# Sample step, block inverse and first memory attention as background jobs beside five projections; value transposes directly behind their projection

## The chip, the cores and the metric

The kernel runs on one core of a Trainium2 chip. The metric is the device time of one execution in microseconds (us). A core has five engines with an instruction queue each: TensorE (PE in the rows; PEld is its weight load), VectorE (DVE), ScalarE (ACT), GpSimd (POOL) and SyncE (SP). Transfers are issued from a queue of SP or ACT.

## What is computed

One step of a decoder trunk of two layers for a prompt of 1024 positions and a sample group of 8 single positions, with the same weights; all 1032 columns go through each projection together, in three chunks of 352, 336 and 344. Layer 0 is the "even" one: gated delta rule (4 heads of 128), dilated attention in windows, and attention over a memory of 256 entries. Layer 1 is the "odd" one: a linear recurrence (RG-LRU) and a memory attention of its own.

```
x0 = prompt and sample
for layer in (0, 1):
    h   = rms_norm(x) * g_pre
    kv  = rms_norm(mem) @ w_mem_kv                  # keys and values of the memory
    mix = concat(branches(h @ w_in), memory_attend(q, kv) * silu(gate))
    x   = x + rms_norm(mix @ w_out) * g_post

# gated delta rule, prompt: chunks of 128
a_low = (beta k k^T) * strict_lower * decay
u, w  = solve(a_low + I, [beta v, beta k exp(g)])   # block inverse, then two levels of joining
for each chunk: v' = u - w S;  o = q S + attn v';  S = decay S + k^T v'

# gated delta rule, sample: one position for each of 8 states
S = exp(g) S;  u = (v - k^T S) beta;  S = S + k u^T;  o = q^T S
```

The outputs are both groups' rows of the last layer, the new states and caches, and the memory's keys and values.

## The kernel before

The kernel is written against a tile framework that schedules: instructions are traced in program order, and each engine's queue is then filled from what is ready, earlier program text first, so that later projections can move ahead of a stalled part. Each engine works its own queue in order. `tc.high_priority(offset=HP)` puts a block ahead of all others. Matrix products of projections are split into three passes of fp32r operands (high x high, low x high, high x low: L164 to L166), 8 blocks of 128 rows each: 24 matmuls for a chunk. A projection is `proj` (weights cast to a high and a low part on ACT and GpSimd, L152 and L154; then, for each chunk, matmuls into a PSUM tile of bank group `p`, the drain that the caller gives, and `tick()`).

`start(lane, steps)` puts a generator on a lane; each `tick()` lets every lane take one portion. What a portion issues is pinned behind the last instruction traced so far on each engine, so that it can't be scheduled earlier than that. `yield n` in a job means a pause of n ticks. `drain_lanes` ticks until the lanes named are empty. `at_once` traces a generator's steps on the spot, unpinned.

The part of layer 0 that matters stands in `even_gdn`'s second half. The preparation of the delta rule writes the chunk matrices to DRAM (`aqd`). Then, in program text: the block inverse of 128 blocks of 32x32 (16 loads `bl` L752 on SP; 31 rows, each with a product `tm` L758 over i*i elements and a sum `xi` L760, both on DVE; a transposed copy L761 and two stores L762 and L763), under high priority; the sample step (convolution of 4 taps, norms, 64 small matmuls `gks` L803, the update `u`, two transposes, and for each of the 8 states a spread `gum` L831 on GpSimd, a matmul `gou` L834, four scalings L837 on ACT, an addition `gst` L838 on DVE and a store L839 issued by ACT; the states are loaded by ACT's queue); the first memory head, `mem_head(0)` (query projection wq00, gate projection wg00, attention `mem_attend` with L375 to L402, store of `mix`); `mem_scaled`, a product for layer 1's memory norm; and three projections taken ahead for the windowed attention, `swa_ahead` (gate wb0, keys/queries ws010 and ws000). These draw their result tiles `pa` from pool `me` under the tags `qm`, `gm`, `mm`, which are also the tags of the attention's query, gate and mix, one buffer each. Drains L520 and L523 are ACT copies into `pa`, L526 is the copy of the sample columns on DVE. After that the bank groups of PSUM are cut anew (L854), and the recurrence proper begins: for each head `chain(h)` loads the inverse from `xd`, joins blocks (`gz` L881, `gt` L886, `gx` L891) and scans the chunks, with the next heads' projections (wq01, wg01, wz0, wq02, ...) beside it.

Layer 1's memory keys and values, `mem_kv(1, ...)`, run at the end of layer 0's output (`out_layer`), beside the norm of the third column chunk (lane "norm2"). For each of four heads a value projection `mv` is drained to a tile `vf` (two buffers, L323), stored, and turned by two transposes L346 and a copy L347 on DVE into `vt`. In layer 1 these turns are a lane of their own, "turn", emptied behind the memory part.

Of the kernel before, what the change touches and what calls it, by code (L numbers as in the profile page):

```python
# [15 lines left out]
P = 128  # L16
# [49 lines left out]
def body(ctx, tc, I, O):  # L66
# [251 lines left out]
    def mem_kv(l, mem, pool, part=None):  # L318
# [17 lines left out]
        for h in range(4 if part != 0 else 0):  # L336
# [13 lines left out]
            if l:  # L350
                start("turn", turn())
            else:
                at_once(turn())
# [201 lines left out]
    def even_gdn(x, prep, sprep):  # L555
        with ExitStack() as es:
# [191 lines left out]
            with tc.high_priority(offset=HP):  # L748
# [6 lines left out]
                V.memset(xi.rearrange("p j i -> p (j i)")[:, 0:1024:33], 1.0)  # L755
                for i in range(1, 32):
                    t3 = tm[:, :i * i].rearrange("p (c j) -> p c j", c=i)
                    V.tensor_tensor(t3, bl[:, 0:i, i][:, None, :].broadcast_to([P, i, i]),  # L758
                                    xi[:, 0:i, 0:i].rearrange("p j c -> p c j"), ALU.mult)
                    V.tensor_reduce(xi[:, i, 0:i], t3, axis=AX.X, op=ALU.add, negate=True)  # L760
                V.tensor_copy(xt.rearrange("p c i -> p i c"), xi)  # L761
                nc.sync.dma_start(out=xd[0].rearrange("h c m j i -> (h c m) (j i)"), in_=xi.rearrange("p j i -> p (j i)"))  # L762
                nc.sync.dma_start(out=xd[1].rearrange("h c m j i -> (h c m) (j i)"), in_=xt.rearrange("p j i -> p (j i)"))  # L763
            nc.scalar.dma_start(out=O["gcp"], in_=gcp)
# [3 lines left out]


            G.tensor_copy(cst_s[:, 3], gpre)  # L770
            nc.scalar.dma_start(out=O["gcs"], in_=cst_s[:, 1:4])
            sc = t3p.tile([P, 12, 8], F32, name="gsc")
            sc2 = t3p.tile([P, 12, 8], F32, name="gsc2")
            wv = vc("gconv", 0, 48).rearrange("p (t j) -> p t j", j=4)
            for j in range(4):
                d = sc if j == 0 else sc2
                V.tensor_tensor(d, cst_s[:, j], wv[:, :, j:j + 1].broadcast_to([P, 12, 8]), ALU.mult)
                if j:
                    V.tensor_tensor(sc, sc, sc2, ALU.add)
            S.activation(sc2, sc, AF.Tanh, scale=0.5)  # L780
            V.scalar_tensor_tensor(sc, sc2, 1.0, sc, ALU.add, ALU.mult)
            V.tensor_tensor(sc2, sc, sc, ALU.mult)
            ps = ctile("gsn")
            T.matmul(ps[:, 0:64], ones, sc2[:, 0:8, :].rearrange("p t b -> p (t b)"), start=True, stop=True)
            nr = t3p.tile([P, 3, 64], F32, name="gnr")
            V.tensor_scalar(nr[:, 0], ps[:, 0:64], 0.25, EPS, op0=ALU.mult, op1=ALU.add)
            rsqrt(nr[:, 1], nr[:, 0], nr[:, 2])
            kq = t3p.tile([P, 4, 8, 2], F32, name="gkq")
            n1 = nr[:, 1].rearrange("p (t b) -> p t b", b=8)
            V.scalar_tensor_tensor(kq[:, :, :, 1], sc[:, 0:4], 0.5 * SC, n1[:, 0:4], ALU.mult, ALU.mult)  # L790
            V.scalar_tensor_tensor(kq[:, :, :, 0], sc[:, 4:8], 0.5, n1[:, 4:8], ALU.mult, ALU.mult)
            ks_ps = ctile("gks")

            sts = []
            for b in range(8):
                t = t3p.tile([P, 4, P], F32, name=f"gst{b}")
                nc.scalar.dma_start(out=t, in_=I["state_gdn"][0, b].rearrange("h k v -> k h v"))
                sts.append(t)
            for b in range(8):
                st = sts[b]  # L800
                for h in range(4):
                    o = (h * 8 + b) * 2
                    T.matmul(ks_ps[:, o:o + 2], st[:, h, :], kq[:, h, b, :], start=True, stop=True)  # L803
            qkp = t3p.tile([P, 4, 8], F32, name="gqkp")
            V.tensor_tensor(qkp, kq[:, :, :, 0], kq[:, :, :, 1], ALU.mult)
            T.matmul(ks_ps[:, 64:96], ones, qkp.rearrange("p h b -> p (h b)"), start=True, stop=True)
            u = t3p.tile([P, 4, 8], F32, name="gu")
            k4 = ks_ps[:, 0:64].rearrange("p (h b t) -> p h b t", h=4, t=2)
            V.tensor_tensor(u, k4[:, :, :, 0], brow[:, 1], ALU.mult)
            V.scalar_tensor_tensor(u, sc[:, 8:12], 0.5, u, ALU.mult, ALU.subtract)  # L810
            V.tensor_tensor(u, u, brow[:, 0], ALU.mult)
            V.tensor_tensor(os_, k4[:, :, :, 1], brow[:, 1], ALU.mult)
            V.tensor_tensor(qkp, u, ks_ps[:, 64:96].rearrange("p (h b) -> p h b", h=4), ALU.mult)
            V.tensor_tensor(os_, os_, qkp, ALU.add)

            rep3 = t3p.tile([P, 2, 3, 4, 8], F32, name="grep3")
            for i in range(3):
                G.tensor_copy(rep3[:, 0, i], kq[:, :, :, 0])
                G.tensor_copy(rep3[:, 1, i], u)
            ps = ctile("grw")  # L820
            for i in range(2):
                T.transpose(ps[0:96, i * P:(i + 1) * P], rep3[:, i].rearrange("p a h b -> p (a h b)"), ident)
            kr_ = t3p.tile([96, P], F32R, name="gkr")
            ur = t3p.tile([96, P], F32R, name="gur")
            V.tensor_copy(kr_, ps[0:96, 0:P])
            V.tensor_copy(ur, ps[0:96, P:256])
            V.tensor_tensor(kr_[64:96], ps[64:96, 0:P], kr_[64:96], ALU.subtract)
            V.tensor_tensor(ur[32:64], ps[32:64, P:256], ur[32:64], ALU.subtract)
            for b in range(8):
                um = t3p.tile([96, 4, P], F32R, name=f"gum{b}", tag="gum", bufs=2)  # L830
                G.tensor_tensor(um, ur[:, None, :].broadcast_to([96, 4, P]),  # L831
                                C("rep32")[0:96, b:32:8][:, :, None].broadcast_to([96, 4, P]), ALU.mult)
                ps = ctile(f"gou{b}")
                T.matmul(ps, kr_, um.rearrange("p h d -> p (h d)"), start=True, stop=True)  # L834
                st = sts[b]
                for h in range(4):
                    S.activation(st[:, h, :], st[:, h, :], AF.Copy, scale=brow[:, 1, h, b:b + 1])  # L837
                V.tensor_tensor(st, st, ps.rearrange("p (h d) -> p h d", h=4), ALU.add)  # L838
                nc.scalar.dma_start(out=O["gdn_s"][b].rearrange("h k v -> k h v"), in_=st)  # L839

            V.tensor_tensor(qkp, os_, os_, ALU.mult)
            ps = ctile("gon")
            T.matmul(ps[:, 0:32], ones, qkp.rearrange("p h b -> p (h b)"), start=True, stop=True)
            V.tensor_scalar(nr[:, 0, 0:32], ps[:, 0:32], 1.0 / 128.0, EPS, op0=ALU.mult, op1=ALU.add)
            rsqrt(nr[:, 1, 0:32], nr[:, 0, 0:32], nr[:, 2, 0:32])
            V.tensor_tensor(os_, os_, nr[:, 1, 0:32].rearrange("p (h b) -> p h b", h=4), ALU.mult)
# [806 lines left out]
```

## Time and profile before

| | |
|---|---|
| three runs | 1916.27, 1918.96, 1923.78 us (median 1918.96) |
| profiled execution | 1920.67 us; span on the core 1918.9 |
| TensorE busy | 1782.3 us, 93% of the span, 11341 matmuls |
| VectorE, ScalarE, GpSimd busy | 1088.6, 715.0, 550.6 us |
| mean granted TensorE clock | 0.954 of full speed |

The profiled execution's time has 1.8 us outside its span. Start times in the rows count from the span's start. [...] In a row on waits: the waiting engine and line, the releaser, total us, times, the longest. In a row in order of time: start, duration, engine, line, operation, output <- inputs, and in brackets the idle time of that engine before it with its releaser.

### The profile page before, as it was taken

How to read it: one execution, taken by the hardware profiler on the slowest of the kernel's cores; microseconds unless marked ns; L12 is line 12 of the kernel's file. 1: busy time of each engine (PE TensorE's matmuls, PEld its weight loads, DVE VectorE, ACT ScalarE, POOL GpSimd, SP SyncE). 2: the span in 40 equal slices, each digit the busy share in tenths (PEclk: the TensorE clock that was granted, in tenths of full speed). 3: DMA queues.
4: the chain of work that ended last, by engine and by line, in shares of the span. 5: the costliest groups of instructions: out<-in, count | busy, mean ns of one | idle time of the engine just before them, and what ended most of it. 6: DMA issues, size and time to landing. Idle time of an engine off the chain costs nothing.

```text
span 1918.9 us, 29175 instructions
## 1 busy us (share of the span) xinstructions
PE 1782.3 (93%) x11341; PEld 1724.7 (90%) x11341; DVE 1088.6 (57%) x2302; ACT 715.0 (37%) x1610; POOL 550.6 (29%) x367
## 2 busy tenths in 40 slices
PE   7999998798999899999999988998499999989996
PEld 6799998698999899999999977998499999988995
DVE  6878759534543314525336376578735647667536
ACT  5355533122322244333333342344223434526432
POOL 3422224222121113231533403215431534331201
PEclk9999998899999899999999998997699999999998
DMA  8435455543344435545644535465633433223554
GB/s 290 180 132 194 181 165 191 193 135 109 114 179 167 177 137 183 205 149 188 213 168 171 169 118 150 131 202 183 234 108 135 143 133 105 84 67 122 152 186 139
DMA packets 160698, 306.25 MB, mean 160 GB/s; under 512 B 25072, under 2 KB 120496, under 8 KB 158640
## 3 DMA queue, kind: packets, MB, share of 16 engines
q1 hardware_dynamic: 67024, 222.47, 33.7%
q10 hardware_dynamic: 93536, 81.93, 13.2%
q8 instruction: 89, 1.46, 0.3%
q14 instruction: 49, 0.40, 0.1%
HBM read 254.05 MB, written 138.28 MB: 204 GB/s over the span
## 4 chain that ended last, share of the span: by engine, by line
PE 73%; DVE 14%; DMA 3%; ACT 3%; issue 2%; ACTq 1%; SPq 0%; POOL 0%; DVEq 0%; POOLq 0%
PE ss L1016 2%; DVE tm L758 1%; PE so L1049 1%; PE mo L401 1%; PE ms L375 1%; PE gz L881 1%; PE gt L886 1%; PE st L1039 1%; DVE xi L760 1%; DVE y L1463 1%; DMA mg<-mixd 1%; DMA mf<-mixd 1%; PE mt L394 1%; DMA gst<-state_gdn 1%; PE svp L1001 1%
## 5 line engine op out<-in xcount | busy, mean ns | idle before, releaser
L1018 DVE CUSTOM_DVE_ANT_0 spr<-ss,cs 128x128 f32<-128x128 f32 (+1 forms) x96 | 32.4, 350 | 90.7 <-PE ss L1016 90.3
L652 DVE SCALAR_TENSOR_TENSOR acc<-pre,vec,acc 128x1024 f32<-128x1024 f32 x36 | 49.2, 1366 | 13.4 <-ACT acc L650 13.2
L1025 ACT ACTIVATE spr<-spr,snm 128x128 f32<-128x128 f32 (+1 forms) x96 | 42.2, 441 | 36.4 <-DVE snm L1020 36.4
L1464 POOL TENSOR_TENSOR y<-y,xr 128x352 f32<-128x352 f32 (+2 forms) x24 | 23.0, 961 | 106.3 <-DVE y L1463 105.8
L381 ACT ACTIVATE pm<-ms,nm 128x256 f32<-128x256 f32 x64 | 29.7, 473 | 49.1 <-DVE nm L379 42.8
L1424 POOL COPY mg<-mixs 128x8 f32<-128x8 f32 x24 | 9.2, 383 | 131.3 <-DVE wo01al L154 48.6
L1409 DVE TENSOR_TENSOR ya<-ya,ysq 128x352 f32<-128x352 f32 (+2 forms) x42 | 26.2, 625 | 32.7 <-ACT ysq L1408 32.5
L1016 PE MATMUL ss<-sw,sw 128*128 128x128 f32 (+1 forms) x192 | 42.4, 322 | 0.0
L1259 DVE TENSOR_SCALAR lacc<-lpre,vec 128x1024 f32<-128x1024 f32 x8 | 19.3, 2418 | 34.0 <-ACT lpre L1249 34.0
L1049 PE MATMUL so<-spt,svt 128*128 128x128 f32 x280 | 38.2, 275 | 0.0
L401 PE MATMUL mo<-mpt,vt 128*128 128x512 f32 x64 | 34.6, 627 | 3.4 <-DVE mpt L396 3.4
L1049 PEld LDWEIGHTS so<-spt,svt 128*128 128x128 f32 x280 | 36.2, 191 | 0.0
L1427 DVE TENSOR_TENSOR mbl<-mg,mbh 128x344 fp32r<-128x344 f32 x24 | 17.2, 715 | 33.3 <-ACT mbh L1426 33.3
L375 PE MATMUL ms<-kt,qm 128*128 128x256 f32 x128 | 33.4, 390 | 0.0
L1262 DVE SCALAR_TENSOR_TENSOR lacc<-lpre,vec,lacc 128x1024 f32<-128x1024 f32 x24 | 32.7, 1363 | 0.3
L375 PEld LDWEIGHTS ms<-kt,qm 128*128 128x128 f32 x128 | 24.6, 198 | 8.9 <-issue 4.9
L1002 DVE COPY svt<-svp 128x512 f32<-128x512 f32 x24 | 15.5, 685 | 28.9 <-PE svp L1001 24.4
L1016 PEld LDWEIGHTS ss<-sw,sw 128*128 128x128 f32 x192 | 31.2, 189 | 0.6 <-DVE sml L1018 0.2
L758 DVE TENSOR_TENSOR tm<-bl,xi 128x1 f32<-128x1 f32 (+30 forms) x31 | 30.3, 976 | 2.5 <-DMA bl<-aqd 2.0
L1272 POOL TENSOR_TENSOR lxl<-lacc,lxh 128x1032 fp32r<-128x1032 f32 x8 | 22.4, 2800 | 30.6 <-ACT lxh L1271 30.6
L1426 ACT CAST mbh<-mg 128x344 fp32r<-128x344 f32 x24 | 11.5, 481 | 52.4 <-DMA mg<-mixd 42.7
L1308 POOL COPY lhl<-lacc 128x1 f32<-128x1 f32 x8 | 4.5, 559 | 89.7 <-DVE lacc L1307 89.7
(2144 smaller groups left out, 7344.8 us busy)
## 6 DMA issues: line engine op xcount, KB each, us to landing
o_sw3s<-cache_swa SPq DMA_DIRECT2D x64, 1023.5 KB
o_sw2s<-cache_swa SPq DMA_DIRECT2D x16, 1022.0 KB
gaq<-aqd ACTq DMA_DIRECT2D x20, 512.0 KB
mf<-mixd SPq DMA_DIRECT2D x19, 344.0 KB
sfb<-fd SPq DMA_DIRECT2D x12, 512.0 KB
aqd<-aq ACTq DMA_DIRECT2D x4, 1024.0 KB
o_sw3p<-sw SPq DMA_DIRECT2D x8, 512.0 KB
mixd<-lgt ACTq DMA_DIRECT2D x8, 512.0 KB
```

What stands on the lines that cost most here:

```text
L375: T.matmul(ps[:, b * 256:(b + 1) * 256], q[:, (b0 + b) * P:(b0 + b + 1) * P], kt[:, h, :], start=True, stop=True)
L381: S.activation(pr[:, b2 * 2 + b, :], ps[:, b * 256:(b + 1) * 256], AF.Exp, bias=nm[:, b0 + b:b0 + b + 1], scale=SC, accum_out=lt[:, b0 + b ...
L401: T.matmul(po, vt[:, kb, h, :], sts[kb], start=kb == 0, stop=kb == 1)
L652: V.scalar_tensor_tensor(acc, pre[:, j:j + 1024], vc("gconv", ti * 4 + j), acc, ALU.mult, ALU.add)
L758: V.tensor_tensor(t3, bl[:, 0:i, i][:, None, :].broadcast_to([P, i, i]), xi[:, 0:i, 0:i].rearrange("p j c -> p c j"), ALU.mult)
L1016: T.matmul(po, q[:, bb * P:(bb + 1) * P], k[:, k0:k0 + w], start=True, stop=True)
L1018: V.tensor_tensor_reduce(pr[:, bb, :w], po, mask, 1.0, NEG, ALU.add, ALU.max, accum_out=ml[:, 0, g, bb:bb + 1])
L1025: S.activation(pr[:, bb, :w], pr[:, bb, :w], AF.Exp, bias=nm[:, bb:bb + 1], scale=SC, accum_out=ml[:, 1, g, bb:bb + 1])
L1049: T.matmul(po[:, (bb % 4) * P:(bb % 4 + 1) * P], vt[:, kb, :], pt[:, o:o + P], start=st, stop=sp_)
L1262: V.scalar_tensor_tensor(acc[:, :1024], pre[:, j:j + 1024], vc("lconv", ti * 4 + j), acc[:, :1024], ALU.mult, ALU.add)
L1409: V.tensor_tensor(acc[:, :n], acc[:, :n], sq[:, :n], ALU.add)
L1464: (V if k % 2 else G).tensor_tensor(yk[k], yk[k], xr[k], ALU.add)
```

## The change

It has two places. In `mem_kv`, layer 1's turns are traced at once behind their value projection, as layer 0's already were, and the emptying of that lane goes. In `even_gdn` three blocks of straight program text become lanes which advance with the ticks of five projections of three chunks each (wq00, wg00, wb0, ws010, ws000):

- "inverse": loads and memsets at the first tick, then a pause of 5, then rows 1-9, 10-14, 15-18, 19-21, 22-24, 25-26, 27-28, 29-30 and 31 with the copy and the stores, one portion a tick (6 to 14). The high priority is gone.
- "sample": convolution; norms and state loads; at tick 4 `gks` and `u`; at tick 6 the transposes and the first spread; then one of the 8 states a tick (7 to 14), each with the next one's spread; the last norm.
- "attend": the first head's attention, in five parts behind the gate projection.

The three projections ahead are now traced before the lanes are emptied, and draw their tiles from `t2` instead of `me` (same tags, other pool). `mem_scaled` comes behind them.

```diff
@@ mem_kv
-            if l:
-                start("turn", turn())
-            else:
-                at_once(turn())
+            at_once(turn())
@@ even_gdn
-            with tc.high_priority(offset=HP):
+            def inverse():
                 for h in range(4):
                     for c in range(4):
                         nc.sync.dma_start(out=bl[...], in_=aqd[...])
                 V.memset(xi, 0.0)
                 V.memset(xi.rearrange("p j i -> p (j i)")[:, 0:1024:33], 1.0)
+                yield 5
                 for i in range(1, 32):
                     ...
                     V.tensor_reduce(xi[:, i, 0:i], t3, axis=AX.X, op=ALU.add, negate=True)
+                    if i in (9, 14, 18, 21, 24, 26, 28, 30):
+                        yield 1
                 V.tensor_copy(xt.rearrange("p c i -> p i c"), xi)
...
+            start("inverse", inverse())
...
+            def sample():
...
+                yield 1
                 ps = ctile("gsn")
...
+                yield 2
                 for b in range(8):
                     ...
                         T.matmul(ks_ps[:, o:o + 2], st[:, h, :], kq[:, h, b, :], start=True, stop=True)
...
+                yield 2
                 ps = ctile("grw")
...
+                spread(0)
+                for b in range(8):
+                    yield 1
+                    if b < 7:
+                        spread(b + 1)
                     ps = ctile(f"gou{b}")
                     T.matmul(ps, kr_, ums[b]...)
                     ...
                     V.tensor_tensor(st, st, ps..., ALU.add)
                     nc.scalar.dma_start(out=O["gdn_s"][b]..., in_=st)
...
+                yield 1
                 ps = ctile("gon")
...
-            mem_head(0)
+            start("sample", sample())
+            q0 = me.tile([P, 1024], F32, name="qm00", tag="qm")
+            mem_query(0, 0, x, I["we"][56], q0)
+            g0 = mem_gate(me, 0, 0, x, I["we"][60])
+            def attend0():
+                mix = me.tile([P, 1024], F32, name="mm00", tag="mm")
+                yield from mem_attend(me, 0, 0, q0, g0, mix)
+                nc.scalar.dma_start(out=mixd[0][:, 8, :], in_=mix)
+            start("attend", attend0())
+            for key in ((0,), (0, 1, 0), (0, 0, 0),):
+                swa_ahead(t3p, x, key)
+            drain_lanes("sample", "attend", "inverse")
             mem_scaled(me)
-            for key in ((0,), (0, 1, 0), (0, 0, 0),):
-                swa_ahead(me, x, key)
@@ out_layer
                 mem_kv(1, mem_reload(pb), np_)
-                drain_lanes("turn")
                 drain_lanes("norm2")
```

## Rows read from the trace of the kernel before

**Rows 1.** The page's busy times: us, share, instructions.
```profile
PE 1782.3 (93%) x11341; PEld 1724.7 (90%) x11341; DVE 1088.6 (57%) x2302; ACT 715.0 (37%) x1610; POOL 550.6 (29%) x367
```

**Rows 2.** Stretches from A on: length, busy us (instructions) by engine, clock, DMA.
```profile
264.50:387.80 123.30, 102.26 (x565) 95.51 (x564) 83.39 (x180) 30.67 (x85) 39.33 (x25) 0.88 0.57 187
300.00:310.00 10.00, 10.00 (x43) 10.00 (x44) 9.55 (x29) 6.07 (x21) 0.51 (x3) 0.50 0.30 109
330.00:350.00 20.00, 8.44 (x32) 6.94 (x33) 19.83 (x19) 2.28 (x4) 8.52 (x6) 0.77 0.27 86
370.00:380.00 10.00, 4.74 (x25) 4.34 (x25) 3.37 (x13) 2.08 (x7) 0.00 (x0) 0.91 0.80 265
387.80:651.00 263.20, 248.38 (x1703) 239.74 (x1702) 117.72 (x346) 72.98 (x197) 53.28 (x26) 0.97 0.42 144
```

**Rows 3.** Stretches of B and behind it, same columns.
```profile
1353.70:1386.00 32.30, 7.58 (x29) 6.25 (x29) 21.65 (x46) 9.70 (x20) 12.44 (x10) 0.56 0.61 222
1386.00:1680.00 294.00, 293.25 (x1813) 285.06 (x1812) 166.60 (x254) 115.54 (x212) 106.98 (x68) 1.00 0.34 116
1400.00:1410.00 10.00, 10.00 (x66) 10.00 (x66) 0.00 (x0) 1.89 (x4) 2.18 (x1) 1.00 0.01 2
```

**Rows 4.** Waits of PE, 264 to 400: us in total, times, longest.
```profile
PE gou L834 <- DVE gst L838: 12.4, 4, 5.8
```

**Rows 5.** All engines in order, 342 to 351: start, us, idle before.
```profile
348.92 1.36 PE L834 MATMUL gou<-gum,gkr 96*128 96x512 f32 x2 [5.81 <-DVE gst L838]
349.29 0.15 DVE L526 COPY sqkv<-ws000p 128x8 f32<-128x8 f32 x1
...
350.08 0.49 PE L164 MATMUL wq01p<-h0h,wq01h 128*128 128x352 f32 x1
```

**Rows 6.** DVE by line, 290 to 352: count, busy us, mean ns.
```profile
L758 DVE TENSOR_TENSOR tm<-bl,xi 128x1 f32<-128x1 f32 (+30 forms) x31 | 30.3, 976 | 2.5 <-DMA bl<-aqd 2.0
L760 DVE TENSOR_REDUCE xi<-tm 128x1 f32<-128x1 f32 (+30 forms) x31 | 15.5, 500 | 0.7
L838 DVE TENSOR_TENSOR gst<-gst,gou 128x512 f32<-128x512 f32 x8 | 5.2, 673 | 0.0
```

**Rows 7.** Waits of ACT, 264 to 400.
```profile
ACT pm L381 <- DVE nm L379: 18.8, 5, 8.7
ACT pa L523 <- DVE mm L402: 13.4, 1, 13.4
...
ACT pa L520 <- DVE gst L838: 10.5, 1, 10.5
```

**Rows 8.** PE in order at the end of B.
```profile
1385.71 0.66 PE L346 MATMUL mvt<-cs,vf 128*128 128x128 f32 x2 [10.10 <-DVE n L1227]
1386.02 0.64 PE L164 MATMUL wq10p<-h1h,wq10h 128*128 128x352 f32 x1
```

**Rows 9.** DVE in order at the end of B.
```profile
1385.15 0.41 DVE L347 COPY vt<-mvt 128x256 f32<-128x256 f32 x1
```

**Rows 10.** ACT in order at the start of B.
```profile
1351.04 0.47 ACT L228 CAST h1h<-hn1hf 128x336 fp32r<-128x336 f32 x1
...
1355.36 0.37 ACT L323 COPY vf<-mv12p 128x256 f32<-128x256 f32 x1 [3.84 <-DMA o_memv<-vf]
...
1356.14 1.04 ACT L152 CAST wx0h<-wx0f 128x1024 fp32r<-128x1024 f32 x1
```

**Rows 11.** Waits of SP's queue, 250 to 300.
```profile
SPq L752 <- DMA gst<-state_gdn: 6.8, 3, 5.2
```

**Rows 12.** DVE's products by shape, 290 to 352.
```profile
L758 DVE TENSOR_TENSOR tm<-bl,xi 128x961 f32<-128x961 f32 x1 | 4.6, 4645 | 0.0
L758 DVE TENSOR_TENSOR tm<-bl,xi 128x625 f32<-128x625 f32 x1 | 3.6, 3616 | 0.0
...
L758 DVE TENSOR_TENSOR tm<-bl,xi 128x676 f32<-128x676 f32 x1 | 1.4, 1370 | 0.0
```

**Rows 13.** Line L831: ns shortest, median, longest; first and last start.
```profile
L831 POOL TENSOR_TENSOR gum<-gur,cs x8: 1045/1910/2270, 319.9 to 343.2; 96x512 fp32r<-96x512 f32 x8
```

More of the change, by code (lines that the diff above doesn't have):

```diff
@@ L763, in even_gdn @@
                 nc.sync.dma_start(out=xd[1].rearrange("h c m j i -> (h c m) (j i)"), in_=xt.rearrange("p j i -> p (j i)"))
+            start("inverse", inverse())
             nc.scalar.dma_start(out=O["gcp"], in_=gcp)
             t3p = pool(s2, "t2")
[L770 to L839, printed above, removed]
```

82 lines of the change are left out of this document (76 added, 6 removed).

## The prediction

> **What bounds the kernel now.** I read the page first. TensorE (PE) is busy 93% of the span [rows 1], so the end moves only by what PE loses: time in which it has nothing it may run, and time at the lower clock. The next view is the table of stretches, cut at the stages that the change touches. In stretch A, from the end of layer 0's preparation to the first matmul of the recurrence (L881), PE is busy 102.26 of 123.30 us at a mean granted clock of 0.88 [rows 2]. It is idle for 21.0 us, and 102.26 x 0.12 = 12.3 us more go with the clock: 33.3 us lost. In stretch B, the end of layer 0 with layer 1's memory keys and values, PE is busy 7.58 of 32.30 us at 0.56 [rows 3]: 24.7 us idle. Behind each stretch PE is nearly full: 248.38 of 263.20 us behind A [rows 2], 293.25 of 294.00 behind B [rows 3]. Work that PE does earlier in A or B is therefore work that it needn't do later, and the gain stays. DMA is no bound, with a share of 0.57 to 0.61 in both [rows 2, 3].
>
> The third view, PE's waits in A, names the value additions of the sample step: the matmul L834 waits 12.4 us for the addition L838, four times [rows 4]. The order in time shows it best. The last two L834 come after 5.81 us of idle at 348.92; ws000's last tail is copied out at 349.29; only then, at 350.08, does the next projection, wq01, begin [rows 5]. DVE was working on the inverse: 31 products L758 (30.3 us) and 31 sums L760 (15.5 us), from 292 to 350, with the eight additions (5.2 us) in between [rows 6]. ACT waits as well: 13.4 us before the copy `pa` L523 for the first attention (both use the same buffer of `me`), 10.5 before the copy L520 for an addition, whose store is queued ahead on ACT [rows 7]. PE starves behind two shared things, DVE and those buffers, not for lack of work.
>
> **Turns (mem_kv).** In B PE's wait of 10.10 us ends at 1385.71, with the second head's transposes, and the first layer 1 projection, wq10, starts at 1386.02 [rows 8]. The copy that frees the transposes' PSUM tile runs at 1385.15 [rows 9], directly behind the last step of the norm, because a lane's portion is pinned behind what DVE was given before. The change unpins it; nothing is added or removed. What can then fill the norm's shadow: wx0's weights are cast at 1356.14, those of wq10 earlier, and their first two column chunks need only norms 0 and 1, whose last cast runs at 1351.04 [rows 10]. That is 2 projections x 2 chunks x 24 matmuls = 96, and at full clock PE does 66 in 10 us [rows 3]: 14.5 us. The third and fourth heads' `mv` must still come out of two buffers `vf`, the third at 1355.36 behind a store's DMA [rows 10], the fourth behind the second head's transposes, which free its buffer; with the copies free that is some 5 us later, about 1361, and 25 us remain for 14.5 us of work. The norm's own small PE steps then queue behind chunks of 3.6 us, but the work that needs the norm comes only after these four. I take **14.5**. Lower bound 8 (the fourth `vf` late, half the chunks fit), upper 24.7 (all idle time, were a third weight in time). Before, layer 1's projections stood behind these transposes in PE's order; the forecast needs them to leave by 1365.
>
> **Inverse.** Its 31 pairs stay: 45.8 us of DVE, plus 5.2 of additions [rows 6]. It loses its priority and comes in nine portions, each behind what DVE was last given, but DVE had been full anyway (19.83 of 20 us, 330 to 350 [rows 2]) with the same content. So the inverse ends about where it did, 350 to 356. The 16 loads L752 keep their place on SP's queue, where 6.8 us had gone with waits for the state loads [rows 11]; those loads now come a tick later, which can win some of it. The loads end one wait of 2.0 us before the first product [rows 6], and five ticks' pause covers that. I cost loads at 0 (from -5 to +3).
>
> The products beside GpSimd are longer than their size says: the one of 625 takes 3.62 us, of 676 1.37, of 961 4.64 [rows 12], and some 6.5 us of the inverse are such excess, estimated by holding the long products against their neighbours in size (for the one of 625 against that of 676, 3.62 - 1.3 = 2.3). GpSimd's spreads L831 (median 1.91 us, eight of them [rows 13]) now come one a portion, so the excess stays; I cost it at 0, within -6 (no excess) and +9 (every spread holds one product up, 8 x 1.91 = 15 us, less the 6.5). [...]
>
> **Sample step and attention.** The 64 small matmuls of `gks`, in one block, hold PE at clock 0.50 from 300 to 310 [rows 2]: 5.0 us. Now they stand between chunks at full clock, so I count **5.0** gained, with up to 2 less. The ahead projections (wb0, ws010, ws000) get buffers of their own in `t2`, so L523's wait for the attention goes; they are interleaved with the eight L834, whose additions come one a tick. The idle time of 330 to 350, 20.00 - 8.44 = **11.6** us [rows 2], is what this removes: ws000 drains some 25 us sooner, and wq01, wg01 and the next ones run under the inverse. With them there, the hole at 370 to 380 (5.3 us) fills as well [rows 2]: **5.3**. Against it stands what is new. An L834 and the attention's transposes now stand in PE's order among chunks, and behind each is a DVE step which waits for a portion with a product of up to 4.64 us [rows 12]. Ten ticks of 3.6 us are 36 us of PE against some 57 of DVE (51.0 [rows 6] and some 6 that the attention and the drains put in between), so PE will meet these waits; before, the longest was 5.81. With the PSUM buffers as slack I take one of that size and a small one, **7** us, between 0 and 22. Sum for A: 5.0 + 11.6 + 5.3 - 7 = **15**, between -18 and 33. Moving the stores of the state and of the first `mix` costs ACT queue time only; ACT is 25% busy here (30.67 of 123.30 [rows 2]).
>
> **Forecast.** 14.5 + 15 = 29.5 off a profiled run of 1920.67 us, 1.7 above the median of 1918.96; from the median, **1889**. Its own range is 1878 to 1903.
>
> **Rivals.**
> Both stretches fill: A gives 26 (the wait of 7 doesn't come, some 4 more of the clock), B 21; 1872. For: there is more than enough hoistable work, since behind A everything is projections and chains. Against: in-order PE between pinned lanes.
> Only the turns pay: A's holes are filled but the pinned steps make as many new ones (22 instead of 7, bound above); 1904. For: DVE has 57 us against 36.
> No change to speak of, the change not doing what it says: norm 2's matmuls and the fourth `vf` keep the projections behind them in B, and A nets nothing; about 1917. For: layer 1's order hung on a queue, which another instruction may take over, such as the wait of 3.84 us for a store in front of `vf` [rows 10].
> Slower: the nine portions wait. Each stands on DVE behind the attention's or an addition's step, and ACT's and DVE's steps of the attention wait for each other today: `pm` for `nm` five times, 18.8 us, 3.8 each [rows 7]. If every portion pays that, 9 x 3.8 = 34 us, the inverse ends at 384 instead of 350, the recurrence starts 34 later, and with the projections run out PE stands still: +33 for A, -14.5 for B, about 1937. It decides from an inverse that ends later than 365, where it eats the turns' gain. For: DVE is full, and the inverse loses its priority. Against: 45.8 us of products fill these waits if a portion is there.
>
> **How the numbers follow.** Chances: forecast 0.49, both fill 0.12, only the turns 0.15, no change 0.13, slower 0.11. A measurement of this kernel tells about 0.5% from no change, so faster is under 1909.4 and slower over 1928.5. The first three give 0.76 less a little of the third's upper end (0.02): faster 0.74; no change and that end 0.15; slower 0.11. The range leaves out the slower case and the lower part of the second: 1868 to 1919.
>
> **What would show it.** In the changed kernel's trace: the transposes' copies L347 come between 1350 and 1365 and wq10 begins more than 15 us before norm 2's last step; if wq10 still starts behind norm 2, the turns are worth nothing. In A: wq01 begins before the inverse's last sum; the copy of ws000's last chunk is 20 us or more ahead of that sum; PE's clock shows no block at 0.50 in `gks`; waits of PE for L838 total under 7 us. The inverse's last sum, counted from its first product, should take 57 to 64 us; 72 or more is the slower rival. [...] What is behind A must not lengthen: if the recurrence's stretch grows by what A gave, PE wasn't its bound and the sum for A fails.

## The result, and the profile after

The changed kernel takes 1891.51 us (median of 6, 1885.63 to 1898.79) beside 1921.37 for the kernel before on the same chip: a ratio of 0.9845, 95% interval 0.9817 to 0.9874. The forecast was 1889, range 1868 to 1919. The profiled execution took 1892.17 us, with a span of 1890.4. The line of the page that answers to [rows 1]:

```profile
PE 1769.7 (94%) x11341; PEld 1714.4 (91%) x11341; DVE 1096.8 (58%) x2302; ACT 714.5 (38%) x1610; POOL 550.4 (29%) x367
```

The same 11341 matmuls in 12.6 us less busy time, and 15.9 us less idle time. Where the time went is read by milestones: the last `kk` of the preparation (start of A), the first `gz` and the last `gf` of the recurrence, the last score `ss` of the windowed attention, the first product `y` on VectorE (L1463, now L1488) in each layer's output and the last one of all, the last matmul of wq10. Each cell is the time from the milestone before it, in us, from one profile of each kernel:

| stage, up to | before | changed | difference |
|---|---|---|---|
| last kk | 264.2 | 263.3 | -0.9 |
| first gz (stretch A) | 123.4 | 126.5 | +3.1 |
| last gf (recurrence) | 263.1 | 248.4 | -14.7 |
| last ss (attention) | 451.3 | 456.8 | +5.5 |
| first y, layer 0 | 171.4 | 167.6 | -3.8 |
| last wq10 (with B) | 132.8 | 119.2 | -13.6 |
| first y, layer 1 | 461.9 | 457.8 | -4.1 |
| last y | 42.8 | 42.8 | 0 |

**Stretch A** didn't get shorter, it got fuller. The stretches of the changed kernel, the first from the last `kk` to the first `gz`, the last one the recurrence. A line has, as in [rows 2], the length, then busy us (instructions) of PE, PEld, DVE, ACT and POOL, the mean granted clock of TensorE as a share of full speed, the busy share of the DMA engines, and GB/s:

```profile
263.30:389.80 126.50, 115.60 (x677) 109.29 (x676) 89.75 (x195) 35.16 (x98) 38.02 (x26) 0.95 0.60 198
290.00:310.00 20.00, 20.00 (x109) 19.97 (x108) 17.27 (x53) 8.63 (x25) 0.60 (x4) 0.66 0.36 149
330.00:350.00 20.00, 19.08 (x117) 17.74 (x115) 19.69 (x22) 2.35 (x5) 9.68 (x4) 1.00 0.51 163
350.00:370.00 20.00, 15.29 (x94) 14.19 (x92) 19.77 (x27) 4.50 (x13) 4.16 (x3) 1.00 0.51 181
370.00:390.00 20.00, 15.93 (x91) 14.23 (x91) 12.78 (x40) 4.03 (x12) 6.44 (x4) 1.00 0.70 229
389.80:638.20 248.40, 230.55 (x1590) 222.13 (x1589) 110.77 (x330) 67.98 (x184) 50.82 (x25) 0.97 0.42 146
```

PE does 677 matmuls ahead of the recurrence where it did 565 [rows 2]. The recurrence (the last row) has 1590 where it had 1703, so what was pulled forward is missing there, and it is 14.7 us shorter. The hole of 330 to 350 is down from 11.6 us to 0.9; 4.7 us of idle at 350 to 370 and 4.1 at 370 to 390 are new or left. The waits of PE from 263 to 392 (total, times, longest), against the 12.4 us of [rows 4]:

```profile
PE wq02p L164 <- ACT qm L492: 3.5, 1, 3.5
PE wz0p L164 <- DVE gms L359: 3.4, 1, 3.4
PE gou L848 <- DVE gst L852: 2.3, 2, 1.3
```

The inverse, though, ends later. DVE in order of time (start, duration; the product and the sum are L757 and L759 now):

```profile
308.19 0.62 DVE L759 TENSOR_REDUCE xi<-tm 128x21 f32<-128x441 f32 x1
...
330.06 1.14 DVE L384 TENSOR_SCALAR pm<-pm,lt 128x256 f32<-128x256 f32 x4
331.12 1.06 DVE L757 TENSOR_TENSOR tm<-bl,xi 128x484 f32<-128x484 f32 x1
...
363.86 1.15 DVE L759 TENSOR_REDUCE xi<-tm 128x31 f32<-128x961 f32 x1
```

From 308.8 to 331.1 it stands still: portion 22 to 24 is pinned behind the attention's steps, the last of which, `pm`, runs directly ahead of it. The last sum ends at 365.0, against 350.5 before. What DVE did from 310 to 330, first before, then in the changed kernel:

```profile
310.00:330.00 20.00, 19.17 (x113) 17.49 (x111) 19.49 (x25) 3.22 (x4) 16.05 (x7) 1.00 0.49 188
```

```profile
310.00:330.00 20.00, 19.23 (x109) 17.39 (x108) 8.79 (x22) 9.35 (x31) 11.81 (x9) 1.00 0.68 243
```

**Stretch B.** PE in order, then the answering copy on DVE, then PE's stretch from 1353 to 1378:

```profile
1350.94 0.66 PE L346 MATMUL mvt<-cs,vf 128*128 128x128 f32 x2 [4.31 <-DVE vt L347]
...
1352.52 0.64 PE L164 MATMUL wq10p<-h1h,wq10h 128*128 128x352 f32 x1
```

```profile
1350.38 0.41 DVE L347 COPY vt<-mvt 128x256 f32<-128x256 f32 x1
```

```profile
1353.00:1378.00 25.00, 25.00 (x152) 24.80 (x151) 12.72 (x33) 7.65 (x16) 5.50 (x5) 0.91 0.47 172
```

wq10 begins at 1352.52 instead of 1386.02 [rows 8], and from then on PE is full, through the whole of norm 2, whose last step ends at 1379.0.

### The profile page after: what moved, and what is told of

It is laid out like the page before. It is cut to its first block, busy times and chain, and to the rows that moved or that the text cites. A ratio compares the mean times of both kernels' runs of the same rounds, so it can differ in the third digit from the quotient of the medians.

```text
span 1890.4 us, 29169 instructions
## 1 busy us (share of the span) xinstructions
PE 1769.7 (94%) x11341; PEld 1714.4 (91%) x11341; DVE 1096.8 (58%) x2302; ACT 714.5 (38%) x1610; POOL 550.4 (29%) x367
## 4 chain that ended last, share of the span: by engine, by line
PE 60%; DVE 11%; DMA 4%; issue 2%; ACT 2%; ACTq 1%; SPq 0%; DVEq 0%; POOL 0%; POOLq 0%
PE ss L1041 2%; PE so L1074 1%; PE ms L372 1%; PE mo L398 1%; PE gz L906 1%; DMA mf<-mixd 1%; PE st L1064 1%; PE gt L911 1%; DVE y L1488 1%; DMA sfb<-fd 1%; DVE y L1489 1%; PE lg L164 0%; PE mt L391 0%; PE lg L166 0%; PE lg L165 0%
## 5 line engine op out<-in xcount | busy, mean ns | idle before, releaser
L649 DVE SCALAR_TENSOR_TENSOR acc<-pre,vec,acc 128x1024 f32<-128x1024 f32 x36 | 49.2, 1367 | 13.4 <-ACT acc L647 13.2
L1041 PE MATMUL ss<-sw,sw 128*128 128x128 f32 (+1 forms) x192 | 43.6, 330 | 4.3 <-DVE sml L1043 4.3
L1434 DVE TENSOR_TENSOR ya<-ya,ysq 128x352 f32<-128x352 f32 (+2 forms) x42 | 26.1, 620 | 31.4 <-ACT ysq L1433 31.2
L1041 PEld LDWEIGHTS ss<-sw,sw 128*128 128x128 f32 x192 | 32.0, 194 | 5.3 <-DVE sml L1043 4.6
L1027 DVE COPY svt<-svp 128x512 f32<-128x512 f32 x24 | 15.5, 686 | 30.4 <-PE svp L1026 25.1
L757 DVE TENSOR_TENSOR tm<-bl,xi 128x1 f32<-128x1 f32 (+30 forms) x31 | 28.1, 905 | 3.6 <-DMA bl<-aqd 2.8
L947 DVE TENSOR_TENSOR guu<-guu,gsc 128x128 f32<-128x128 f32 x28 | 8.0, 286 | 35.9 <-PE gsc L946 35.7
L1068 ACT COPY spt<-st 128x384 f32<-128x384 f32 (+2 forms) x48 | 22.5, 477 | 16.7 <-PE st L1064 16.5
```

The source lines that it names most:

```text
L649: V.scalar_tensor_tensor(acc, pre[:, j:j + 1024], vc("gconv", ti * 4 + j), acc, ALU.mult, ALU.add)
L1041: T.matmul(po, q[:, bb * P:(bb + 1) * P], k[:, k0:k0 + w], start=True, stop=True)
L1434: V.tensor_tensor(acc[:, :n], acc[:, :n], sq[:, :n], ALU.add)
```

## Experiments

Ratios are to the kernel before, with 95% intervals. Lines of code in the edits are those of the kernel that was edited.

### The two halves apart

`e1_turns`, the kernel before with the turns alone:

```diff
-            if l:
-                start("turn", turn())
-            else:
-                at_once(turn())
+            at_once(turn())
...
-                drain_lanes("turn")
```

> The kernel before with the turns alone traced at once. The two traces differ by 20.3 us across stretch B (layer 1's first convolution products start 26.9 us sooner, of which 10.5 us are older than B, and their last 30.7). Theory: B's gain is independent of A, so about -18 to -21 us against before, wq10 starting some 15 us or more ahead of norm 2's last step. Rival: B's gain needs the earlier state that A brings, or only shows with it; then it is under 10 us.

Measured: 1899.95 us, 0.9907 (0.9878 to 0.9937), 19.4 us by the medians, 20.8 by the spans (1918.9 to 1898.1). The stage up to the last wq10 takes 119.9 us (before 132.8), that up to layer 1's output 454.9 (461.9). wq10 starts 28.0 us ahead of norm 2's last step. The theory holds; the turns' gain needs nothing from A.

`e2_lanes`, the changed kernel with this part undone:

```diff
-            at_once(turn())
+            if l:
+                start("turn", turn())
+            else:
+                at_once(turn())
...
+                drain_lanes("turn")
```

> The changed kernel with the turns back in their lane, so stretch A's lanes alone. Theory: the gain of A as the two traces show it at the start of layer 0's output, 10 to 11 us against before, and the hole of B back at some 25 us of idle. Rival: A's gain is given back in the windowed attention, whose last product came only 7.0 us sooner; then 7 us or less.

Measured: 1914.96 us, 0.9983 (0.9959 to 1.0006). The interval reaches from 8 us faster to 1 slower. The profiled run is the fastest of the 12, with a span 10.6 us below that of before; from the last `kk` to the last `gf` it takes 372.9 us, before 386.5. By the runs the first theory's 10 us is too much, and the rival's bound of 7 fits, though not its reason: the attention took 452.1 us here against 451.3, so it gave nothing back in this profile. The hole of B is back, with 22.0 us of idle in front of wq10 (24.7 before).

### What in stretch A pays

`e4_buffers`, the kernel before with its three projections ahead on buffers of their own, nothing else:

```diff
             for key in ((0,), (0, 1, 0), (0, 0, 0),):
-                swa_ahead(me, x, key)
+                swa_ahead(t3p, x, key)
```

> The kernel before with one edit: the three projections ahead draw their tiles from a pool of their own instead of the attention's. Theory: ACT's wait of 13.4 us for the attention's buffer was a cause of A's holes, and this alone gives 4 to 9 us. Rival: the holes come from DVE, busy with the inverse in front of the additions; then 0 within 2 us, and the idle time of 330 to 350 us stays near 11.6.

Measured: 1913.28 us, 0.9963 (0.9939 to 0.9986): 7 us, beside 4 by the medians for the lanes and buffers together (`e2_lanes`); the two intervals overlap. PE's waits for the additions L838 fall from 12.4 to 5.6 us, and the hole of 330 to 350, columns as before, from 11.6 to 8.6, so the rival's sign, a hole near 11.6, didn't come, though most of the hole stays:

```profile
330.00:350.00 20.00, 11.45 (x37) 9.73 (x38) 19.76 (x20) 2.18 (x4) 9.70 (x6) 0.59 0.64 200
```

ACT's waits from 264 to 400:

```profile
ACT pa L520 <- PE ws000p L164: 15.1, 1, 15.1
...
ACT pa L523 <- DVE sgs L362: 4.0, 1, 4.0
```

The wait of L523 for the attention, 13.4 us [rows 7], is gone; for other steps of DVE it now waits 4.0. L520 now waits for PE's own matmuls, 15.1, where it waited 10.5 for an addition.

`e5_turns_buffers`: both edits, `e1_turns` and `e4_buffers`, on the kernel before. No lanes.

> The kernel before with two edits: the turns at once, and the projections ahead on tiles of their own; no lanes for inverse, sample step and attention. Alone the turns gave 0.9907 and the buffers 0.9963 of before, the lanes with the buffers 0.9983. Theory 1, the buffers and the turns are all of the change's gain and the lanes add nothing: 0.985 to 0.987, the same as the changed kernel beside it. Theory 2, the lanes carry a part of stretch A's gain of their own (the traces' lines stand 10.6 us apart at layer 0's output for the lanes with the buffers, 7.5 for the buffers alone): 3 us or more slower than the changed kernel.

`e8_change` is the changed kernel itself, on the same chip beside it.

> The changed kernel itself once more, on the same chip as the three others, as their measure. Expected 0.985 of before, as in the first comparison (0.9845, 0.9817 to 0.9874).

Measured: 1893.82 us, 0.9854 (0.9826 to 0.9882), without lanes; 1894.64 us, 0.9862 (0.9835 to 0.9889), the change. The same. Theory 1 holds: two small edits, turns and buffers, are the gain, and making lanes of the inverse, the sample step and the attention adds nothing that these runs can tell (each interval is some 5 us to either side). The hole is still there without lanes, columns as before, with PE's waits from 263 to 400:

```profile
330.00:350.00 20.00, 8.69 (x29) 7.21 (x29) 19.73 (x21) 2.08 (x4) 11.85 (x7) 0.70 0.62 202
```

```profile
PE gou L831 <- DVE gst L835: 5.9, 2, 4.8
PE ws000p L164 <- DVE sqkv L523: 4.3, 1, 4.3
```

So the lanes do fill it, and lose as much elsewhere. From the last `kk` to the last `gf`: before 386.5, buffers 381.9, turns and buffers 377.4; with lanes 374.9 (changed), 375.5 (`e8_change`) and 372.9 (`e2_lanes`). The lanes are 2 to 9 us ahead there. The attention then takes 450.7 and 451.6 us without lanes, 456.8, 459.3 and 452.1 with them, so that what is lost there is lost in two of three profiles.

### Does the inverse's end matter?

`e3_inv_first`, the changed kernel with the inverse out of its lane and under priority again:

```diff
-            start("inverse", inverse())
+            with tc.high_priority(offset=HP):
+                at_once(inverse())
...
-            drain_lanes("sample", "attend", "inverse")
+            drain_lanes("sample", "attend")
```

> The changed kernel with the block inverse out of its lane: unpinned and under high priority, as before the change; sample step, attention, buffers and turns as in the changed kernel. In the changed kernel the inverse stands still from 308.8 to 331.1 us behind the attention's steps and ends at 365.0 instead of 350.5. Theory 1, the pinned portions cost time: the last sum ends near 350 again, the recurrence's first product moves from 389.8 to about 376, and the whole is 4 to 9 us faster than the changed kernel. Theory 2, PE alone bounds this stretch: PE did 110 more matmuls there meanwhile, the inverse's end doesn't matter, within 2 us of the changed kernel. Theory 3, the inverse in one block starves the attention and the additions: 3 to 10 us slower.

Measured: 1934.29 us, 1.0081 (1.0049 to 1.0113), slower than before and some 43 us slower than the changed kernel. Theory 3 in kind, at four times the upper price that it named. DVE in order of time, then the small matmuls (ns shortest, median, longest; first and last start):

```profile
337.95 1.03 DVE L762 COPY xtt<-xi 128x1024 f32<-128x1024 f32 x1
338.84 0.40 DVE L781 TENSOR_TENSOR gsc<-cst_s,vec 128x96 f32<-128x96 f32 x2
```

```profile
L809 PE MATMUL gks<-gkq,gst x64: 352/352/374, 345.9 to 359.3; 128*128 128x2 f32 x64
```

The inverse is done at 339, some 27 us sooner than in the changed kernel, and only then does the sample step take its first step on DVE. The sample step's lane pins its first portion behind what DVE was last given, and that is the inverse's last copy here; `gks`, the additions, the lanes tied to them and the recurrence (first `gz` 427.2) follow. So this run delays the sample step as well and doesn't set the inverse's end alone.

`e6_inv_earlier` and `e7_inv_filler` are two milder ways: the pause shortened, and the rows unpinned and without priority, behind the projections in the program.

```diff
-                yield 5
+                yield 2
```

> The changed kernel with the inverse's pause cut from 5 ticks to 2, so that its portions stand at ticks 3 to 11 instead of 6 to 14. Theory 1, the 22 us in which the inverse stands still behind the attention's steps are what holds the recurrence's start at 389.8: more rows run ahead of the attention, the last sum comes at 345 to 355 instead of 363.9, the recurrence starts 5 to 12 us sooner, and the whole is 2 to 6 us faster than the changed kernel. Theory 2, the portions then stand in front of the sample step's small steps, as the whole inverse did when it had priority (gks at 345.9 instead of 289.8, 43 us slower than the changed kernel): slower than the changed kernel by 5 us or more.

```diff
-                yield 5
+                return
+                yield
+            def rows():
                 for i in range(1, 32):
...
-                    if i in (9, 14, 18, 21, 24, 26, 28, 30):
-                        yield 1
...
-            start("inverse", inverse())
+            at_once(inverse())
...
-            drain_lanes("sample", "attend", "inverse")
+            drain_lanes("sample", "attend")
+            rows()
```

> The changed kernel with the inverse's rows traced straight, unpinned and without priority, behind the five projections: DVE's queue then has them wherever nothing earlier in the program is ready. The loads stay where they are. Sample step and attention stay lanes. Theory 1, it is the pinning of the portions that leaves DVE idle while the inverse waits: the inverse ends at 335 to 350, the recurrence starts 8 to 14 us sooner than at 389.8, and the whole is 3 to 8 us faster than the changed kernel. Theory 2, PE bounds the stretch and its projections are only moved about: within 2 us of the changed kernel.

Measured: 0.9933 (0.991 to 0.9957) and 0.9909 (0.9882 to 0.9936), 14 and 10 us slower than `e8_change` beside them. The last sums start at 357.0 and 348.1, up to 16 us sooner than in the changed kernel, and yet the recurrence starts later, at 401.7 and 403.1 instead of 389.8 (394.6 in `e8_change`). For `e6_inv_earlier` theory 1's last sum of 345 to 355 didn't come, and theory 2 had the time but not the place: `gks` starts at 289.7, as in the changed kernel. For `e7_inv_filler` both theories failed. The waits of PE, first of `e6_inv_earlier`, then of `e7_inv_filler`, and ACT in order of time in `e7_inv_filler`:

```profile
PE mt L391 <- ACT gz0t L355: 11.3, 1, 11.3
```

```profile
PE wz0p L164 <- DVE gz L357: 12.3, 1, 12.3
```

```profile
375.62 0.34 ACTq L305 DMA_DIRECT2D memd<-mss  x1
...
377.98 0.35 ACTq L305 DMA_DIRECT2D memd<-mss  x1
378.37 3.01 ACTq L894 DMA_DIRECT2D gaq<-aqd  x5
...
393.62 0.47 ACT L378 ACTIVATE pm<-ms,nm 128x256 f32<-128x256 f32 x1 [16.15 <-DMA gXT<-xd]
```

The recurrence's loads `gaq` and `gX` are issued by ACT's queue, behind the stores of the steps before. They leave at 378.4 here, 27 us after the inverse is done; in the changed kernel at 371.6, 5 us after. The activations behind these issues wait 16.15 us for a load (11.39 in the changed kernel), and PE with them. What they come closely behind each time is the sample step: in all fourteen profiles they leave 1.8 to 8.5 us behind the start of its last matmul, `gon` (358.1 in `e5_turns_buffers`, 369.0 in the changed kernel, 371.7 in `e7_inv_filler`). Behind the inverse's last copy they leave anything from 2.4 us (`e11_both`) to 64 (`e3_inv_first`: copy done at 339.0, `gon` at 397.7, loads at 403.2). So an earlier end of the inverse alone doesn't bring the recurrence forward here. That the sample step's end would is not shown, since no run moves it by itself, and from the loads to the recurrence's first matmul there are another 18 to 29 us, whose spread is open.

### What is left of the holes

Three kernels on the base of `e5_turns_buffers`, and the two edits on the changed kernel. `e9_queues`:

```diff
-                V.tensor_copy(sqkv[:, h, c, g, :], ps[:, npr:n])
+                S.copy(sqkv[:, h, c, g, :], ps[:, npr:n])
...
-                nc.scalar.dma_start(out=O["gdn_s"][b]..., in_=st)
+                nc.sync.dma_start(out=O["gdn_s"][b]..., in_=st)
```

> Turns and own buffers without lanes (the kernel that ran at 0.9854 of before), with two steps taken off queues on which something waits: the sample columns' copies of the windowed projections go from DVE to ACT, and the eight stores of the sample step's states from ACT's queue to SP's. In the kernel it is made from, PE stood idle for 11.3 us between 330 and 350 us: ws000 waited 4.3 us for such a copy on DVE, behind one product of the inverse, wq01 2.7 us for another, and ACT's copies waited 15 and 15.8 us behind stores that wait for an addition. Theory 1, these queues are what is left of A's holes: the idle time of 330 to 350 falls under 5 us, and the whole comes to 0.980 to 0.983 of before. Theory 2, the additions on DVE hold L831 anyway, or the recurrence's start (383.8) is set by the sample step's end: idle time moves, within 2 us of 0.9854.

`e10_scaled_later`:

```diff
-            mem_scaled(me)
...
                     mem_head(h + 1)
+                    if h:
+                        mem_scaled(me)
```

> The same base kernel (turns and own buffers without lanes) with one edit: the two products `mss` on GpSimd, which lie beside the inverse there, are traced some 100 us later, in the recurrence. In the base the product of 576 on DVE takes 8.57 us beside them and a weights' low part, against 1.25 in the kernel before and 1.24 in the changed kernel. Theory 1, the stretch on DVE follows the GpSimd instruction that reads SBUF: the product of 576 falls below 4 us, all 31 together by 5 us or more, and the last sum comes by 349 instead of 354.2. In time 0 to -4 us, as PE is bound by other waits as well. Theory 2, the long products come from something else: their sum stays within 2 us.

`e11_both`: both on the base.

> Both edits of the two kernels above on the same base. Theory: the two add up; 0.977 to 0.982 of before, the fastest of the series. Rival: the recurrence's first product doesn't come before 380, because its loads stand behind the sample step's end, and the time is that of the base, 0.985.

`e12_change_both`: both on the changed kernel.

> The changed kernel, lanes and all, with the same two edits. Theory, the lanes are worth nothing beside free queues and buffers: no faster than both edits without the lanes (within 3 us of it, or slower, since the inverse's end at 364 stays). Rival, the lanes pay once ACT's and DVE's queues are free: 4 us or more faster than without them.

Measured: 0.988 (0.985 to 0.991), 0.9851 (0.9817 to 0.9885), 0.9854 (0.9826 to 0.9882) and 0.9863 (0.9829 to 0.9898). Each lies within the interval of its base. In `e9_queues` the idle time of 330 to 350 went from 11.3 to 8.65 us, not under 5, and the wait for the additions went from 5.9 to 10.7:

```profile
330.00:350.00 20.00, 11.35 (x45) 10.52 (x46) 19.73 (x16) 1.91 (x4) 6.89 (x6) 0.58 0.76 249
```

```profile
PE gou L831 <- DVE gst L835: 10.7, 2, 8.6
```

Theory 2: one wait took the place of another, and DVE, full here at 19.73 of 20, is the releaser in both. `e11_both` has the recurrence start at 377.8, the earliest of all and before the 380 of its rival, and is no faster; `e12_change_both` says once more that the lanes add nothing to free queues. No version beat the change.

The product of 576 elements, first in `e5_turns_buffers`, then in `e10_scaled_later`:

```profile
L755 DVE TENSOR_TENSOR tm<-bl,xi 128x576 f32<-128x576 f32 x1 | 8.6, 8570 | 0.0
```

```profile
L755 DVE TENSOR_TENSOR tm<-bl,xi 128x576 f32<-128x576 f32 x1 | 1.7, 1674 | 0.0
```

With `mss` gone from beside it the product is short again, as theory 1 has it; that the reads of `mss` are the cause isn't shown. It takes 8.57 to 8.72 us in the three kernels with `mss` there (`e4_buffers`, `e5_turns_buffers`, `e9_queues`), 1.67 and 1.68 in the two without (`e10_scaled_later`, `e11_both`). All 31 together fell from 32.9 to 29.2 us, 3.7 and not 5, while the product of 841 took 4.66, against 1.58 in `e5_turns_buffers`; the last sum came at 350.7, not by 349.

## Why the prediction was right, and where it wasn't

The total was right, 29.9 us by the medians where 29.5 was forecast. Its two halves were off in opposite directions, and one of them for a wrong reason: by the runs of each half alone the turns gave 19.4 us and not 14.5, stretch A 4.4 (interval -1 to 8) and not 15. That the sum came within half a microsecond is luck, and the second measurement of the same kernel gives 26.1.

**Turns: right mechanism, term too small.** 14.5 us were forecast, 13.6 + 4.1 = 17.7 came by the stages and 19.4 by the runs of the turns alone. The term that was mis-sized is the number of matmuls that fit: I counted the first two chunks of two projections, 96. Up to the end of norm 2's last cast `h1h`, at 1378.1, the changed kernel does 129 projection matmuls (139 with the turns alone, up to its own at 1388.6): 22 more because chunk 2's blocks follow the norm block by block, and 11 (21) because the third projection, wx1, was in time as well. 129 matmuls at 66 in 10 us [rows 3] are 19.5 us. That wx1 could be in time stood in the prediction as the upper bound only; the trace of before had shown its cast on ACT 22 us ahead of the norm's end:

```profile
1363.05 1.03 ACT L152 CAST wx1h<-wx1f 128x1024 fp32r<-128x1024 f32 x1
```

Norm 2 did slip behind the chunks, by some 4 us (its last cast ends 6.3 us sooner, and the products `y` ahead of it began 10.7 sooner), and cost nothing, as forecast. The `vf` tiles weren't late.

**Inverse: wrong.** "The inverse ends about where it did, 350 to 356": it didn't. It ended at 365.0, and took 73.6 us from its first product, beyond the 72 that was to be the mark of the slower rival. The step that failed is "DVE had been full anyway": DVE's work is the same, but pinning made it wait with nothing to do, 8.79 of 20 us busy from 310 to 330 where it had been 19.49. The first half of the slower rival came true, then. Its second half, PE running out of projections, didn't: 112 matmuls more were at hand, and the recurrence began only 2.2 us later. (That rival books A at -33, which the prediction's own lower bound for A, -18, leaves out, and no terms are shown from which -18 follows.)

**Clock of the small matmuls: wrong.** 5.0 us were booked because the `gks` matmuls would stand between chunks. PE in order, in the changed kernel:

```profile
289.69 0.32 PE L166 MATMUL ws010p<-h0h,ws010l 128*128 128x336 f32 x1
289.84 11.33 PE L808 MATMUL gks<-gkq,gst 128*128 128x2 f32 x64
...
302.25 0.48 PE L166 MATMUL ws010p<-h0h,ws010l 128*128 128x336 f32 x1
```

The lane moves all 64 in one portion, so they are one block still. It begins at full clock, behind full-speed projections (1.00 from 280 to 290), and the granted clock of 290 to 310 is 0.66, against 0.67 in the same window before; the next projection starts at the lower level (0.48 us for one matmul, 0.32 ahead of the block). The diff shows a single pause ahead of the loop and none in it. I read the lane's name, not its pauses. The clock gave something back all the same, where the sum had no term for it: from 330 to 390 it is 1.00 throughout now, where it had been 0.77 from 330 to 350 and 0.91 from 370 to 380 [rows 2].

**Buffers and holes: right in sum, wrongly shared out.** The 11.6 us of 330 to 350 went (0.9 left). The 5.3 us at 370 to 380 didn't fill; holes of 4.7 and 4.1 us lie in 350 to 390 now. The new waits for L838 are 2.3 us, well under the 7 allowed. Over A and the recurrence the changed kernel wins 386.5 - 374.9 = 11.6 us, forecast 15: 7.1 us of PE's idle time (35.9 to 28.8) and 4.5 of its busy time (350.6 to 346.2, for as many matmuls), beside a clock in A of 0.95 instead of 0.88. But the experiments give most of the effect on the whole to the buffers: 7 us alone, and the change's whole effect together with the turns. In the prediction the buffers were half a sentence, with no price of their own, and the rival "only the turns pay" didn't part them from the lanes.

**Given back later: not foreseen.** The attention is 5.5 us longer, though the change doesn't touch it; the sum had "the gain stays". In the changed kernel most of it is one place, the merging of the three dilations (DVE L1134 to L1137, GpSimd beside it, the scores L1041 behind it):

```profile
774.96 2.62 DVE L1134 TENSOR_TENSOR snum<-snum,sfb 128x1024 f32<-128x1024 f32 x1 [1.54 <-DMA sfb<-fd]
777.62 3.91 DVE L1136 TENSOR_TENSOR snum<-snum,snum 128x1024 f32<-128x1024 f32 x1
781.57 3.26 DVE L1137 TENSOR_TENSOR snum<-snum,sg 128x1024 f32<-128x1024 f32 x1
```

```profile
773.30 6.42 POOL L418 TENSOR_TENSOR mc01k<-mc01k,mqb 128x1024 f32<-128x1024 f32 x2 [7.03 <-DMA mqb<-qmd]
779.68 4.07 POOL L154 TENSOR_TENSOR ws200l<-ws200f,ws200h 128x1024 fp32r<-128x1024 f32 x1
```

```profile
785.09 2.93 PE L1041 MATMUL ss<-sw,sw 128*128 128x256 f32 x6 [4.30 <-DVE sml L1043]
```

In the kernel before the same three took 2.16, 2.01 and 1.22 us; GpSimd stood idle beside the first two and began a product `mc01k` at 792.63, beside the third:

```profile
788.36 2.16 DVE L1109 TENSOR_TENSOR snum<-snum,sfb 128x1024 f32<-128x1024 f32 x1 [1.59 <-DMA sfb<-fd]
790.55 2.01 DVE L1111 TENSOR_TENSOR snum<-snum,snum 128x1024 f32<-128x1024 f32 x1
792.60 1.22 DVE L1112 TENSOR_TENSOR snum<-snum,sg 128x1024 f32<-128x1024 f32 x1
```

They are 4.4 us longer, PE stands 4.3 us, and the clock is at 0.50 from 783.9 to 790.7, around the end of the hole. Over the whole attention PE's idle time is 3.7 us more than before and its busy time 1.9. That is what this profile shows; it isn't tied to the lanes, since `e9_queues` to `e11_both` have an attention of 455.5 to 457.1 us without lanes and `e2_lanes` one of 452.1 with them. What decides it, perhaps the moment at which GpSimd's work meets DVE's, isn't shown, since none of the runs set it, and why layer 0's output then takes 3.8 us less stays open.

**GpSimd beside the products: right in size, not in its reason.** I took the excess as unchanged at 6.5 us within -6 and +9, with one spread for each portion. The 31 products took 28.1 us, 2.2 less than before; the least of any run is 24.5 (`e7_inv_filler`), so before had at least 5.8 on top, and 3.6 are left. But seven of the eight spreads L831 (L839 now) ran from 309.9 to 323.5, in the inverse's pause, and met no product; the long product is now that of 676 with 4.23 us, beside the eighth spread, a weights' low part (341.32) and the start of `mss` (343.69). Nor does the trace of before show the excess at the spreads: the products of 529, 576 and 676 ran beside them in 1.36, 1.25 and 1.37 us (in the changed kernel 529 and 576 took 1.14 and 1.24 with GpSimd idle), while the long ones lay beside `mss` (484, 2.22 us) or a weights' low part (625 and 961 [rows 12]). So the upper end of +9, in which every spread holds one product up, was an estimate that these two traces don't bear out. In ten profiles (before, changed, `e3_inv_first` to `e5_turns_buffers`, `e7_inv_filler` to `e11_both`) the 31 sums took 15.5 to 15.6 us each time, the products between 24.5 and 34.2.

## What to carry to other kernels

Before making background jobs of steps, look for the plain reason for the wait: here the result tiles of three projections shared their buffers with the attention, and one transposed copy was pinned behind a norm; undoing these two is worth the whole change. A step pinned behind whatever its engine was last given inherits the waits of that work: an engine that was full can stand idle with its work at hand (here the inverse stood for 22.3 us, and DVE did 11.0 us of other work in them), and the pinned piece ends later although nothing was added. Whether that later end costs anything is a question of its own; here the recurrence's loads came behind another piece. A gain in one stage is worth what is left of it at the end, so put milestones through the whole profile and take the difference stage by stage before a term of the sum is called confirmed.

## What was not expected of the hardware

One VectorE product of 576 elements took 1.25, 8.57 and 1.67 us in three kernels (before, `e5_turns_buffers`, `e10_scaled_later`), the 8.57 beside two GpSimd products `mss` of 1024 elements and a weights' low part; the 7.3 us on top of this one instruction are about what the whole inverse carried before. And during 64 matmuls of two columns, with PE shown busy for 10.00 of 10 us, the granted clock, 1.00 when they began, fell to a mean of 0.62 in the stretch from 290 to 300. Here a busy share of 100% didn't tell that the clock was kept; the clock's own column did.
